# A hybrid decoder step: token tiles that overlap by 15 in the pooling mixer, compact 32x32 inverses, and an uneven final block

## The chip, the core and the metric

One core of a Trainium2 chip runs the kernel. The core has a matrix engine (TensorE, in the profile PE, with its weight loads as PEld), a vector engine (VectorE, DVE), a scalar engine (ScalarE, ACT), GpSimd (POOL), and SyncE (SP), whose queue issues the DMA transfers here. PE multiplies a stationary operand of up to 128 by 128 (the weights, loaded ahead of each product) with a moving operand and writes to PSUM, which has eight banks here. The metric is the time of one execution in microseconds of device time.

## What is computed

The reference is one step of a two-layer decoder, D = 1024, for 512 prompt tokens and 8 x 8 sample tokens (64), so T = 576 columns. All of it is float32. Cut to what matters:

```python
def pool_mixer(h, buf, w_grp, scale, n_past):
    # group g: trailing mean over POOL_WINDOWS[g] = 2, 4, 8, 16 positions minus the token,
    # then a linear map of the group's 256 channels, and a scale per channel
    ...
    diffs.append(total / count - cur[..., c0:c1])
    y = einsum('blgc,gce->blge', d, w_grp).reshape(B, L, D_MODEL)
def swiglu(h, w_in, w_out):
    gu = h @ w_in
    return (silu(gu[..., :D_FF]) * gu[..., D_FF:]) @ w_out      # D_FF = 2816
# layer 0: x += norm(pool_mixer(norm(x)));       x += norm(swiglu(norm(x)))
# layer 1: x += norm(gated_delta_net(norm(x)));  x += norm(swiglu(norm(x)))
```

A token's pooled mean needs at most the 15 tokens before it. In the gated delta net (16 value heads, chunks of 64 tokens) each chunk needs the inverse of a triangular matrix, which is built from 32x32 blocks. Besides the outputs for prompt and sample tokens, the last 15 mixer inputs, the last convolution inputs and the delta-rule states are returned.

## The kernel before, in words

The residual x is kept transposed, channels on partitions and tokens in columns, as eight tiles of 128 x 576. Weights and activations are split into a high and a low part (wh, wl; hH, hL; aH, aL; dH, dL in the mixer), both of a reduced float32 type, and each product is three: wh by the high part, wh by the low part, wl by the high part (mm3, line 979). ACT makes the high part of a weight, DVE or POOL the low one (line 971 and after; wraw is the loaded tile). Products of plain F32 operands show as two records each.

The work runs in this order.

- Mixer (from line 1227). Five token tiles are loaded (xt; four of 128 prompt tokens and one of 64 sample tokens), normed (xn), and transposed into x (residual, line 1303). The difference of mean and token is a product of xn with a band matrix: bm for a token tile, bf for the first one, bh (15 columns wide) for the tokens of the tile before that reach into this one, bs for the sample tokens and bt for their saved state rows (stp). Two halves of columns, 256 and 320 (HALVES), one in PSUM banks A and one in B; for each the four window groups one after the other (loop from line 1320).
- FFN of layer 0 (ffn, from line 1148). The gate and up products of six blocks of 128 features run for the halves 256 and 320 (gate_up), so that the second half's norm can follow; the other blocks use a Strassen scheme on halves of 288 and 288 (EVEN; its operands are ta, tb, s1h, dh and so on). The output products (out, line 1173) run after each of four blocks of features; the last block goes half by half, since the norm of a half needs all its outputs.
- Gated delta net: four groups of four heads; each is projected (ps_m), convolved, and goes through a scan with the inverses (inv32, line 1407), while the projections of the next group run. Uw holds the triangular matrices, ia and ii are the working tiles of the inverse; vt is read back from DRAM (z_d).
- FFN of layer 1, whose last block ends the kernel: the outputs yo are squared and summed (nsq, nacc), scaled with a gain (nh), turned back to token rows by PE transposes (turn_y, line 2165; yT), and added to the turned residual x (xa, xb) by a scaling on DVE with the norm's factor nrc (finish1, line 2182). PIECES says which token rows are turned together, up to 128.

The order of the instructions on all engines comes from a planner (class Plan). It records every operation with a cost from a formula, schedules the list forward and backward, and then shakes the ranks window by window with the seeds in the table CHOSEN. So any change in the operations needs a new table, and gives a new order everywhere. The planner also places filler products (ps_w, ones by ones, line 527) where it foresees that PE waits. EITHER (line 827) leaves it to the planner whether DVE or POOL does an operation. The banks of PSUM are handed out by tag in rings (RING): "A" is banks 0, 1, 2 and "B" is 3, 4, 5.

All instructions that the planner emits have one line in the profile (531, in the changed kernel 526), so the tiles' names tell them apart.

## Time and profile before

| what | us |
|---|---|
| median of 3 runs | 1526.5 (1526.38 to 1527.4) |
| profiled execution | 1525.06 |
| its span, first to last instruction | 1523.3 |
| PE busy in the span | 1501.0 |
| DVE busy | 1155.7 |
| ACT busy | 840.6 |
| POOL busy | 129.4 |

In a row of a timeline stand start, duration, engine, line, operation, out<-in with the sizes (partitions x elements), and in brackets an idle time ahead of it with what ended it. The duration of a product holds its latency; how fast products follow each other is read from their starts. In a row of a group stand the sum and the mean in ns. "x2" counts instructions that were put into one row, and the weight loads of PE have rows of their own.

### The profile page before, as it was taken

To read this page: it belongs to the slowest core of one execution; us is meant where nothing else is said; L and a number is where in the kernel's file an instruction comes from. 1 tells how busy PE (TensorE), PEld (TensorE's weight loads), DVE (VectorE), ACT (ScalarE), POOL (GpSimd) and SP (SyncE) were. 2 spreads that over 40 slices of the span, in tenths; PEclk is the share of its full clock that TensorE was granted. 3 is DMA by queue.
4 is the path that set the end of the run, shared out by engine and by line. 5 is a ranking of instruction groups with operands and counts; after the bars stand their busy time and mean duration, and the time that the engine had idled before them with its cause. 6 is when DMAs were issued, how large, how long until landed. Compare 5 with 4: busy or idle time off the path is not lost.

```text
span 1523.3 us, 30379 instructions
## 1 busy us (share of the span) xinstructions
PE 1501.0 (99%) x11850; PEld 1452.8 (95%) x11850; DVE 1155.7 (76%) x2284; ACT 840.6 (55%) x1815; POOL 129.4 (8%) x269
## 2 busy tenths in 40 slices
PE   8999999999999999999999999999999999999997
PEld 7999999999999899899899899999999999999997
DVE  6993566678688698997899799667896476766865
ACT  7753543435466975764763764545565453534553
POOL 4210000000011010121120120100110000000000
PEclk9999999999999999999999999999999999999999
DMA  6563323233457433335433544657765333233263
GB/s 190 156 188 110 98 74 111 67 99 104 148 170 204 114 88 111 102 103 147 111 112 93 147 127 128 202 158 220 240 184 155 109 87 96 83 89 110 66 196 99
DMA packets 344902, 197.86 MB, mean 130 GB/s; under 512 B 13547, under 2 KB 337740, under 8 KB 344751
## 3 DMA queue, kind: packets, MB, share of 16 engines
q1 hardware_dynamic: 344759, 195.92, 44.6%
q8 instruction: 93, 1.52, 0.4%
q14 instruction: 50, 0.41, 0.1%
HBM read 165.60 MB, written 30.52 MB: 129 GB/s over the span
## 4 chain that ended last, share of the span: by engine, by line
PE 88%; DVE 6%; ACT 3%; DMA 2%; issue 1%; POOL 0%; SPq 0%; DVEq 0%; ACTq 0%; POOLq 0%
PE ps_B L531 29%; PE ps_A L531 26%; PE ps_m L531 19%; PE ps_s L531 5%; PE ps_k L531 5%; PE ps_x L531 2%; PE ps_e L531 1%; DVE wl L531 1%; PE ps_n L531 1%; DVE Uw L531 1%; DMA vt<-z_d 1%; DVE ac L531 1%; ACT wh L531 1%; DMA wraw<-in_gdn_w_in_dram 0%; DMA yo<-y_d 0%
## 5 line engine op out<-in xcount | busy, mean ns | idle before, releaser
L531 ACT ACTIVATE wh<-wraw 128x1024 fp32r<-128x1024 f32 (+4 forms) x239 | 232.5, 978 | 201.5 <-PE ps_B L531 79.6
L531 DVE TENSOR_TENSOR wl<-wraw,wh 128x1024 fp32r<-128x1024 f32 (+4 forms) x231 | 258.3, 1122 | 76.0 <-ACT wh L531 40.3
L531 PE MATMUL ps_m<-hH,wh 128*128 128x320 f32 (+1 forms) x832 | 251.5, 313 | 0.0
L531 PE MATMUL ps_m<-hL,wh 128*128 128x320 f32 (+1 forms) x832 | 247.5, 306 | 0.1
L531 PE MATMUL ps_m<-hH,wl 128*128 128x256 f32 (+1 forms) x832 | 245.8, 308 | 0.1
L531 PEld LDWEIGHTS ps_m<-hH,wh 128*128 128x128 f32 x832 | 155.1, 190 | 4.0 <-issue 1.0
L531 PEld LDWEIGHTS ps_m<-hL,wh 128*128 128x128 f32 x832 | 156.0, 190 | 2.0 <-issue 0.8
L531 PEld LDWEIGHTS ps_m<-hH,wl 128*128 128x128 f32 x832 | 154.7, 190 | 1.7 <-issue 0.4
L531 PE MATMUL ps_B<-hH,wh 128*128 128x320 f32 (+1 forms) x444 | 127.8, 304 | 0.2
L531 PE MATMUL ps_B<-hL,wh 128*128 128x320 f32 (+1 forms) x444 | 127.1, 304 | 0.0
L531 PE MATMUL ps_B<-hH,wl 128*128 128x320 f32 (+1 forms) x444 | 127.1, 304 | 0.0
L531 PE MATMUL ps_A<-hH,wh 128*128 128x256 f32 (+1 forms) x432 | 119.4, 292 | 0.0
L531 PE MATMUL ps_A<-hL,wh 128*128 128x256 f32 (+1 forms) x432 | 117.7, 290 | 0.0
L531 PE MATMUL ps_A<-hH,wl 128*128 128x256 f32 (+1 forms) x432 | 117.5, 291 | 0.1
L531 PE MATMUL ps_B<-aL,wh 128*128 128x288 f32 x352 | 100.0, 296 | 0.0
L531 PE MATMUL ps_B<-aH,wl 128*128 128x288 f32 x352 | 99.2, 297 | 0.7 <-DVE wl L531 0.7
L531 PE MATMUL ps_B<-aH,wh 128*128 128x288 f32 x352 | 99.1, 298 | 0.5 <-DVE xa L531 0.5
L531 PE MATMUL ps_A<-aL,wh 128*128 128x288 f32 x352 | 98.3, 296 | 0.0
L531 PE MATMUL ps_A<-aH,wl 128*128 128x288 f32 x352 | 97.7, 297 | 0.0
L531 PE MATMUL ps_A<-aH,wh 128*128 128x288 f32 x352 | 97.1, 297 | 0.0
L531 PEld LDWEIGHTS ps_B<-hH,wh 128*128 128x128 f32 x444 | 81.7, 188 | 0.7 <-ACT wh L531 0.6
L531 DVE SCALAR_TENSOR_TENSOR ac<-u,cwt,ac 128x600 f32<-128x600 f32 x96 | 79.5, 837 | 3.3 <-ACT ac L531 3.1
(463 smaller groups left out, 4040.8 us busy)
## 6 DMA issues: line engine op xcount, KB each, us to landing
wraw<-in_ffn_w_in_dram SPq DMA_DIRECT2D x77, 512.0 KB
wraw<-in_gdn_w_in_dram SPq DMA_DIRECT2D x56, 512.0 KB
graw<-in_ffn_w_in_dram SPq DMA_DIRECT2D x33, 512.0 KB
wraw<-in_ffn_w_out_dram SPq DMA_DIRECT2D x32, 448.0 KB
wraw<-in_gdn_w_out_dram SPq DMA_DIRECT2D x24, 512.0 KB
wraw<-in_ffn_w_out_dram SPq DMA_DIRECT2D x32, 320.0 KB
St<-in_state_gdn_rec_dram SPq DMA_DIRECT2D x32, 256.0 KB
out_dram<-St SPq DMA_DIRECT2D x32, 256.0 KB
```

Of the source, the lines that this page charges most:

```text
L531: calls[e](*a, **k)
```

## The change

Three parts, and a new table CHOSEN with them.

1. The mixer's token tiles overlap. Tile i starts at prompt token 0, 113, 225, 338 or 448 (TILES: start, rows that only serve as history, new tokens); the last holds 64 prompt rows and the 64 sample rows. Every new token has its 15 predecessors in its own tile, so bh goes, and bs now makes the columns of the last tile, 49 prompt and 64 sample tokens. The halves of the mixer, and of the first FFN's gate and up products, become 240 and 336 (MIX). Per channel tile there are six band products instead of nine.
2. In inv32, the four transposes of 32 partitions on DVE at each end become four copies on ACT and one DVE transpose over 128 partitions, in two different orders of the two steps.
3. In the last block of the second FFN the halves are 320 and 256 (LAST), in five pieces of rows instead of six. All its output products use the banks A, and all turned y the banks B; before, the first half had outputs in A and turned y in B, and the second the other way round.

```diff
@@ -28,10 +28,13 @@
 T = SEQ + SMP
 Half = collections.namedtuple("Half", "i o n")
 HALVES = (Half(0, 0, 256), Half(1, 256, 320))
+MIX = (Half(0, 0, 240), Half(1, 240, 336))
+TILES = ((0, 0, 128), (113, 15, 112), (225, 15, 113), (338, 15, 110), (448, 15, 113))
 EVEN = (Half(0, 0, 288), Half(1, 288, 288))
 EV = 288
 KQ = NC // 2
-PIECES = (((0, 128), (128, 128), (256, 32)), ((288, 128), (416, 96), (512, 64)))
+LAST = (Half(0, 0, 320), Half(1, 320, 256))
+PIECES = (((0, 128), (128, 128), (256, 64)), ((320, 128), (448, 128)))
 DFF = 2816
 FBLOCKS = ((6, 5, 4, 7), (5, 5, 5, 7))
 AB = 7
@@ -77,207 +80,199 @@
     CHOSEN = (
-        "0: 51633 4180 93590 78750 34477 23530 63076 77272 88530 16072 91213 50029 90818 92607 6488 48788 652 "
...
+        "0: 21739 22500 52758 86855 86637 95893 57905 59345 46358; 1: 98229 52998 77840 70450 66207 3734 98530 "
...
@@ -1173,7 +1168,8 @@
         def out(bi, f0, m, hf, w):
             s = state[hf.i]
             at = slice(hf.o, hf.o + hf.n)
-            ps = bank("AB"[hf.i])[:, :hf.n]
+            ends = turn is not None and bi == len(blocks) - 1
+            ps = bank("A" if ends else "AB"[hf.i])[:, :hf.n]
             mm3(ps, w, lambda k: tuple(v[:, at] for v in acts[f0 + k]), blocks[bi])
@@ -1216,7 +1212,7 @@
                         out(bi, f0, m, hf, w)
-                for hf in EVEN:
+                for hf in EVEN if turn is None else LAST:
                     for m in range(NC):
                         out(bi, f0, m, hf, wts.load(wout, f0 * P, m * P, nb))
                     finish(hf, state[hf.i]["acc"])
@@ -1234,10 +1230,12 @@
             def load_x(tt):
-                n = P if tt < SPANS else SMP
-                xts[tt] = ip.tile([P, D], F32, name="xt", tag="xt", bufs=3)[:n]
-                SP.dma_start(xts[tt], x_prompt[0, tt * P:(tt + 1) * P] if tt < SPANS
-                                  else x_sample.rearrange("b t d -> (b t) d"))
+                t0 = TILES[tt][0]
+                n = min(P, SEQ - t0)
+                xts[tt] = ip.tile([P, D], F32, name="xt", tag="xt", bufs=3)
+                SP.dma_start(xts[tt][:n], x_prompt[0, t0:t0 + n])
+                if n < P:
+                    SP.dma_start(xts[tt][n:], x_sample.rearrange("b t d -> (b t) d"))
@@ -1262,18 +1260,16 @@
-                h_ = ip.tile([P, POOL_BUF], F32, name="bh%d" % g)
-                POOL.memset(h_, 1.0 / win)
-                POOL.affine_select(h_, h_, [[-1, POOL_BUF]], ALU.is_ge, 0.0, base=win - 1 - P, channel_multiplier=1)
-                bh.insert(0, h_)
             for g in (3, 2, 1, 0):
                 win = 2 << g
-                s_ = ip.tile([SMP, SMP], F32, name="bs%d" % g)
-                DVE.tensor_tensor(s_.rearrange("p (b t) -> p b t", b=NB),
-                                  bm[g][:SMP, :SMP].rearrange("p (b t) -> p b t", b=NB),
-                                  seqm.unsqueeze(2).to_broadcast([SMP, NB, NT]), op=mult)
+                s_ = ip.tile([P, P - POOL_BUF], F32, name="bs%d" % g)
+                EITHER.tensor_copy(s_[:, :SMP - POOL_BUF], bm[g][:, POOL_BUF:SMP])
+                POOL.memset(s_[:SMP, SMP - POOL_BUF:], 0.0)
+                DVE.tensor_tensor(s_[SMP:, SMP - POOL_BUF:].rearrange("p (b t) -> p b t", b=NB),
+                                  bm[g][SMP:, SMP:].rearrange("p (b t) -> p b t", b=NB),
+                                  seqm2[SMP:].unsqueeze(2).to_broadcast([SMP, NB, NT]), op=mult)
@@ -1286,27 +1282,26 @@
...
+                n = min(P, SEQ - TILES[tt][0])
+                DVE.tensor_scalar(xn[:n], xt[:n], st_[:n], None, op0=mult)
+                if n < P:
+                    DVE.scalar_tensor_tensor(out=xn[n:], in0=xt[n:], scalar=st_[n:], in1=grow[n:], op0=mult, op1=mult)
+                    SP.dma_start(np_sample[0, :, POOL_BUF - NT:POOL_BUF], xn[n:])
             def residual(tt, hi):
-                n = P if tt < SPANS else SMP
+                t0, r, n = TILES[tt]
                 for c4 in range(0, NC, 4):
                     px = bank("AB"[hi], (P, 4, P))
                     for c in range(4):
-                        PE.transpose(px[:, c, :n], xts[tt][:, (c4 + c) * P:(c4 + c + 1) * P], ident[:n, :n])
-                    ACT.activation(x[:, c4:c4 + 4, tt * P:tt * P + n], px[:, :, :n], AF.Copy)
+                        PE.transpose(px[:, c], xts[tt][:, (c4 + c) * P:(c4 + c + 1) * P], ident)
+                    ACT.activation(x[:, c4:c4 + 4, t0 + r:t0 + r + n], px[:, :, r:r + n], AF.Copy)
@@ -1352,20 +1348,20 @@
                         ps = bank(tag)
-                        for tt in mine[:2]:
-                            o = tt * P - o0
-                            PE.matmul(ps[:, o:o + P], xns[tt][:, cs], bm[g] if tt else bf[g], start=True, stop=tt == 0)
-                            if tt:
-                                PE.matmul(ps[:, o:o + POOL_BUF], xns[tt - 1][:, cs], bh[g], start=False, stop=True)
+                        for tt in mine:
+                            t0, r, k = TILES[tt]
+                            o = t0 + r - o0
+                            band = bf[g] if tt == 0 else bs[g] if tt == SPANS else bm[g][:, r:r + k]
+                            PE.matmul(ps[:, o:o + k], xns[tt][:, cs], band, start=True, stop=tt < SPANS)
+                        if hi == 1:
+                            PE.matmul(ps[:, np_:n], stp[:, cs], bt[g], start=False, stop=True)
                         gn = prm[:, G_MPRE + c:G_MPRE + c + 1]
-                        ACT.activation(dH[:, j, :256], ps[:, :256], AF.Copy, scale=gn)
-                        DVE.scalar_tensor_tensor(out=dL[:, j, :256], in0=ps[:, :256], scalar=gn,
-                                                 in1=dH[:, j, :256].bitcast(F32), op0=mult, op1=sub)
+                        ACT.activation(dH[:, j, :np_], ps[:, :np_], AF.Copy, scale=gn)
+                        DVE.scalar_tensor_tensor(out=dL[:, j, :np_], in0=ps[:, :np_], scalar=gn,
+                                                 in1=dH[:, j, :np_].bitcast(F32), op0=mult, op1=sub)
                         if hi == 1:
-                            PE.matmul(ps[:, 256:n], xns[SPANS][:, cs], bs[g], start=True, stop=False)
-                            PE.matmul(ps[:, 256:n], stp[:, cs], bt[g], start=False, stop=True)
-                            ACT.activation(dH[:, j, 256:], ps[:, 256:n], AF.Copy)
-                            DVE.tensor_tensor(dL[:, j, 256:], ps[:, 256:n], dH[:, j, 256:].bitcast(F32), op=sub)
+                            ACT.activation(dH[:, j, np_:], ps[:, np_:n], AF.Copy)
+                            DVE.tensor_tensor(dL[:, j, np_:], ps[:, np_:n], dH[:, j, np_:].bitcast(F32), op=sub)
@@ -1410,11 +1406,12 @@
         XT = ap_.tile([P, 2, 512], F32, name="ii", tag="ii", bufs=1)
+        D32 = XT[:, 1].rearrange("p (i h) -> p i h", h=16)
         for b in range(4):
             s = slice(32 * b, 32 * b + 32)
-            DVE.transpose(A[s], W[s, :, 32 * b:32 * b + 32].rearrange("p h i -> p i h").unsqueeze(2)
-                          .to_broadcast([32, 32, 2, 16]))
-            yield 1.2
+            ACT.activation(D32[s], W[s, :, s].rearrange("p h i -> p i h"), AF.Copy)
+        DVE.transpose(A, D32.unsqueeze(2).to_broadcast([P, 32, 2, 16]))
+        yield 1.2
         EITHER.tensor_copy(X, eye2)
         for m in range(31, 0, -1):
@@ -1423,10 +1420,10 @@
             DVE.tensor_tensor(X[:, :m, lo:], X[:, :m, lo:], tv, op=sub)
             yield 2 * (m * (16 - lo) + 60) / 700
+        DVE.transpose(XT[:, 1].rearrange("p (i j) -> p i j", j=32), X.rearrange("p j i -> p i j"))
         for b in range(4):
             s = slice(32 * b, 32 * b + 32)
-            DVE.transpose(W[s, :, 32 * b:32 * b + 32].rearrange("p h (i d) -> p i d h", d=2),
-                          X[s].rearrange("p j i -> p i j"))
+            ACT.activation(W[s, :, s].rearrange("p h i -> p i h"), D32[s], AF.Copy)
             yield 0.6
@@ -2168,10 +2165,10 @@
...
             for i, (o, n) in enumerate(PIECES[hf.i]):
                 if c % 4 == 0:
-                    yT[o, c // 4] = bank("BA"[hf.i], (P, 4, P))[:n].rearrange("p c f -> p (c f)")
+                    yT[o, c // 4] = bank("B", (P, 4, P))[:n].rearrange("p c f -> p (c f)")
                 ps = yT[o, c // 4]
@@ -2184,22 +2181,23 @@
...
-            last = PIECES[hf.i][2][1]
+            whole = hf.n // P
-                n = n if i == 2 else P
-                a = acc[0]
-                PE.matmul(ps[:n, i:i + 1], a[:, i * P:i * P + n] if i < 2 else a[:, EV - n:], ones[:, 0:1],
-                          start=True, stop=True)
-            for r, q in ((slice(0, P), slice(0, 2)), (slice(0, last), slice(2, 3))):
-                ACT.activation(rc[r, q], ps[r, q], AF.Sqrt, bias=eps_c[r], scale=1.0 / D)
-                DVE.reciprocal(rc[r, q], rc[r, q])
+                PE.matmul(ps[:n, i:i + 1], acc[0][:, o - hf.o:o - hf.o + n], ones[:, 0:1], start=True, stop=True)
+            for r, q in ((slice(0, P), slice(0, whole)), (slice(0, hf.n % P), slice(whole, whole + 1))):
+                if r.stop:
+                    ACT.activation(rc[r, q], ps[r, q], AF.Sqrt, bias=eps_c[r], scale=1.0 / D)
+                    DVE.reciprocal(rc[r, q], rc[r, q])
...
```

The rest is of the same kind: ffn takes its halves as an argument (the second one keeps 256 and 320), and the last 15 prompt rows come from the last tile.

The order of instructions moves with it. First PE in the middle of the last block, where the first half of the outputs ends and the second starts. Before:

```order
L531 MATMUL ps_n_3745<-ones,nacc 128x1 x2
L531 MATMUL ps_B<-ident,nh 128x128
L531 MATMUL ps_n_3745<-ones,nacc 32x1
L531 MATMUL ps_B<-ident,nh 128x128
L531 MATMUL ps_B<-ident,nh 32x128
L527 MATMUL ps_w<-ones 128x128 x5
L531 MATMUL ps_B<-ident,nh 128x128 x2
L531 MATMUL ps_B<-ident,nh 32x128
L531 MATMUL ps_B<-ident,nh 128x128 x2
L531 MATMUL ps_B<-ident,nh 32x128
L527 MATMUL ps_w<-ones 128x128 x2
L531 MATMUL ps_B<-aH,wh 128x288
```

After, from the last products of the first half (320 columns) on; before these rows 256-wide products stand mixed with 320-wide ones from 25 rows earlier on:

```order
L526 MATMUL ps_A<-aH,wl 128x320
L526 MATMUL ps_A<-aH,wl 128x256 x2
L526 MATMUL ps_A<-aH,wh 128x256 x2
L526 MATMUL ps_A<-aL,wh 128x256 x2
L526 MATMUL ps_B<-ident,nh 128x128
L526 MATMUL ps_A<-aH,wl 128x256 x2
L526 MATMUL ps_A<-aH,wh 128x256
L526 MATMUL ps_B<-ident,nh 128x128
L526 MATMUL ps_A<-aH,wh 128x256
L526 MATMUL ps_B<-ident,nh 64x128
```

The filler products (ps_w) are gone here, and the transposes of nh stand between products of the second half; the norm products (ps_n<-ones,nacc) of the first half come some 60 rows later.

Then DVE at the first of the four inverses. Before, and after:

```order
L531 STREAM_TRANSPOSE ia<-Uw 32x1024
L531 TENSOR_TENSOR QD<-ps_k,QD 128x2x128
L531 STREAM_TRANSPOSE ia<-Uw 32x1024 x3
L531 TENSOR_TENSOR ks<-ps_k,ks 64x128
L531 TENSOR_TENSOR ii<-ia,ii 128x31
L531 TENSOR_TENSOR ks<-ps_k,ks 64x128
L531 TENSOR_TENSOR ii<-ii 128x31
```

```order
L526 TENSOR_TENSOR vt<-ps_x,nk 128x4x128
L526 STREAM_TRANSPOSE ia<-ii 128x1024
L526 TENSOR_TENSOR ks<-ps_k,ks 64x128
L526 TENSOR_TENSOR ii<-ia,ii 128x31
L526 COPY nct<-u 128x24
L526 TENSOR_TENSOR ii<-ii 128x31
```

Four transposes into ia are one, and its source is now ii, which ACT has filled with four copies of 32x512 from Uw.

Last PE where the mixer turns from the first half of the columns (banks A) to the second (banks B). Before:

```order
L531 MATMUL ps_A<-dL,wh 128x256
L531 MATMUL ps_A<-dH,wl 128x256
L531 MATMUL ps_A<-dL,wh 128x256
L531 MATMUL ps_A<-dH,wl 128x256
L531 MATMUL ps_B<-bm_142,xn 128x128
L531 MATMUL ps_B<-bh_144,xn 128x15
L531 MATMUL ps_B<-bm_142,xn 128x128
L531 MATMUL ps_B<-bh_144,xn 128x15
L527 MATMUL ps_w<-ones 128x128 x2
L531 MATMUL ps_B<-bs_154,xn 128x64
L531 MATMUL ps_B<-bt_155,stp 128x64
L531 MATMUL ps_B<-bs_154,xn 128x64
```

After:

```order
L526 MATMUL ps_B<-bm_142,xn 128x113
L526 MATMUL ps_B<-bm_142,xn 128x110
L522 MATMUL ps_w<-ones 128x128 x4
L526 MATMUL ps_n_235<-ones,nacc 128x1 x2
L526 MATMUL ps_B<-ident,xt 128x128 x8
L522 MATMUL ps_w<-ones 128x128 x2
L526 MATMUL ps_n_238<-ident,nrc 128x128
L526 MATMUL ps_n_238<-ident,nrc 128x112
L526 MATMUL ps_B<-bm_142,xn 128x113
L526 MATMUL ps_B<-bm_142,xn 128x110
L522 MATMUL ps_w<-ones 128x128 x5
L526 MATMUL ps_B<-bs_150,xn 128x113 x2
```

Before, the band products of the second half stood among products of the first, with two fillers ahead of the sample products; now none of them stands there, and 11 of 14 new fillers stand in these rows, three more just behind them.

## The prediction

> **What bounds the kernel now.** I read the page first (busy shares, then the chain that ended last), then the busy time by 40 us windows, then the filler products by stage, and last the rows of the places that the change touches.

> ```profile
> PE 1501.0 (99%) x11850; PEld 1452.8 (95%) x11850; DVE 1155.7 (76%) x2284; ACT 840.6 (55%) x1815; POOL 129.4 (8%) x269
> PE 88%; DVE 6%; ACT 3%; DMA 2%; issue 1%; POOL 0%; SPq 0%; DVEq 0%; ACTq 0%; POOLq 0%
> ```

> TensorE (PE) is busy nearly all the time, and 88% of the chain is its own work. So time can come from two places only: fewer or cheaper products, and the stretches where PE has nothing to do. The windows show where those stretches are (columns: length, then PE busy, weight loads, DVE, ACT, POOL, then the granted clock; the 520 us row is the delta net as a whole).

> ```profile
> 0.00:40.00 40.00, 34.34 (x233) 31.71 (x234) 27.02 (x78) 30.08 (x74) 18.82 (x78) 0.91 0.65 181
> 40.00:80.00 40.00, 39.94 (x322) 39.05 (x321) 38.28 (x89) 28.92 (x61) 8.39 (x9) 1.00 0.61 182
> 440.00:960.00 520.00, 513.34 (x4344) 479.87 (x4342) 458.66 (x1086) 334.36 (x913) 83.24 (x161) 1.00 0.44 125
> 760.00:800.00 40.00, 39.63 (x283) 37.87 (x283) 38.23 (x96) 27.14 (x73) 9.71 (x16) 1.00 0.37 107
> 1240.00:1280.00 40.00, 40.00 (x304) 39.99 (x303) 24.39 (x42) 14.45 (x22) 0.00 (x0) 1.00 0.31 90
> 1480.00:1520.00 40.00, 33.69 (x250) 31.16 (x248) 23.93 (x42) 19.91 (x39) 0.00 (x0) 1.00 0.34 106
> ```

> The FFN windows such as 1240 to 1280 are full: only the product count and width matter there. The start loses 5.7 us, the end 6.3 us (and the tail after it), and the delta net 6.7 of 520, some tenths in each window, with DVE at 38 of 40 in the fuller ones. Busy time also hides waiting, because the plan puts filler products (ps_w) where it expects PE to wait. By stage:

> ```profile
> 0.00:80.00 80.00, 3.62 (x16) 3.16 (x16) 0.96 0.63 181
> 440.00:960.00 520.00, 7.72 (x48) 6.72 (x48) 1.00 0.44 125
> 1480.00:1523.30 43.30, 3.06 (x20) 2.68 (x20) 0.96 0.35 109
> ```

> An F32 product is two records, so these are 8, 24 and 10 fillers, which are waits that do no work.

> **The change, part by part.** The sum is made against the profiled execution (1525.06 us, span 1523.3), which is 1.4 us below the median of the three runs, 1526.5; I add the sum to the median.

> *Mixer.* The 24 products over a second tile (bh) go, and the eight sample products (bs), 64 rows deep before, become 128 deep and 113 wide. Rows (start, duration):

> ```profile
> 31.58 0.43 PE L531 MATMUL ps_B<-bs,xn 64*128 64x64 f32 x2
> 31.94 0.44 PE L531 MATMUL ps_B<-bt,stp 120*128 120x64 f32 x2
> 32.19 0.39 PE L531 MATMUL ps_B<-dH,wh 128*128 128x320 f32 x1
> 33.96 0.29 PE L531 MATMUL ps_B<-bh,xn 128*128 128x15 f32 x2
> 34.09 0.47 PE L531 MATMUL ps_B<-bm,xn 128*128 128x128 f32 x2
> 34.32 0.39 PE L531 MATMUL ps_B<-dL,wh 128*128 128x320 f32 x1
> ```

> From start to start a bh takes 0.13 us, a bm 0.23, a bs 0.36. So 24 x 0.13 = 3.1 us go with the bh, and 8 x (0.36 - 0.23) = 1.0 with the bs, if it now costs what a bm does. The narrower bm I leave at their price. Wider transposes of the last tile give back about 0.3 (eight of 128 by 128, 0.11 each, for eight of 64). So 3.8 us of PE work go. But the order now plans 25 fillers up to the second half of the first FFN against 8: 14 of them stand where the first half of the mixer has ended and the second waits for its band matrices and its last token tile, 4 where the FFN turns to its second half. At the price of a filler, 0.22 us (two records; their spacing is shown below), the 17 more are 3.7 us. The shorter work is planned to end up as waiting, since norms, copies and splits on ACT (30.08 of 40 us) and DVE (38.28) set when operands are ready; ten small instructions more (bs copies, memsets, the last tile's norm) go to DVE and POOL ahead of it. Net -0.1; bounds: -3.8 if the waits turn out empty, +4 if each lasts twice its fillers and the work saved is no help.

> *Halves 240 and 336 instead of 256 and 320*, in 48 mixer and 288 FFN pairs. No product of this 3-term kind narrower than 256 columns is in the trace. Its neighbours:

> ```profile
> 65.09 0.28 PE L531 MATMUL ps_A<-hH,wh 128*128 128x256 f32 x1
> 65.81 0.28 PE L531 MATMUL ps_A<-hH,wh 128*128 128x256 f32 x1
> 44.15 0.31 PE L531 MATMUL ps_B<-dH,wl 128*128 128x320 f32 x1
> 45.03 0.34 PE L531 MATMUL ps_B<-dL,wh 128*128 128x320 f32 x1
> 1513.72 0.73 PEld L531 LDWEIGHTS ps_n<-ones,nacc 128*128 128x128 f32 x6
> ```

> Six steps each: 0.72 us for 256 columns (120 ns), 0.88 for 320 (147 ns); at 288 the window 1240 to 1280 has 304 in 40 us (132 ns). That is a line of 0.42 ns a column, so 336 takes 153.7 and 240 takes 113.3 ns, together the same 267 as before. The other bound is that 120 is a floor: +6.7 ns x 336 = +2.3 us. The last row shows weight loads (0.19 each) about 108 ns apart, (0.73 - 0.19) / 5, which is under 113, so I lean to the line: +0.5, range 0 to +2.3.

> [...]

> *Compact inverses*, four times (one for each head group):

> ```profile
> L531 DVE STREAM_TRANSPOSE ia<-Uw 32x1024 f32<-32x1024 f32 x16 | 32.6, 2034 | 0.2
> L531 DVE STREAM_TRANSPOSE Uw<-ii 32x512 f32<-32x512 f32 x16 | 18.2, 1138 | 0.4
> L531 ACT ACTIVATE Rs<-ps_k 32x512 f32<-32x512 f32 x8 | 4.7, 589 | 8.3 <-PE ps_k L531 8.1
> L531 DVE TENSOR_TENSOR wl<-wraw,wh 128x1024 fp32r<-128x1024 f32 x151 | 184.4, 1225 | 39.4 <-ACT wh L531 22.9 <-PE ps_B L531 7.8 <-PE ps_A L531 7.2
> L531 POOL TENSOR_TENSOR wl<-wraw,wh 128x1024 fp32r<-128x1024 f32 x8 | 19.3, 2414 | 18.5 <-ACT wh L531 18.5
> DVE vt L531 <- DMA vt<-z_d: 12.4, 4, 5.2
> ```

> DVE loses 50.8 us and gets 4 x (2.03 + 1.14) = 12.7 back if a transpose over 128 partitions costs what one over 32 does (four times as much at the other end, then it wins nothing: the columns decide in the rows, 1024 against 512, so I take the first). It also takes the eight weight splits from POOL, 8 x 1.23 = 9.8. Net -28 us on DVE. ACT gets 32 copies of 32x512, 32 x 0.59 = 19 us. The chain of one inverse gets 4 x 2.03 + 4 x 1.14 = 12.7 before to 3.2 + 8 x 0.59 = 7.9, nearly 5 us shorter. PE is hidden behind none of this directly: it works on projections meanwhile. What it can win is its waits from 440 to 960. The new order plans 12 fillers there instead of 24, 12 x 0.22 = -2.7 us, and I take that. Bounds: +4 (a new order meets its waits elsewhere, ACT's copies delay a weight's high part, wh, for which DVE's wl and then PE wait), and -8 (fillers and half the open waits go). Not all can go: vt waits for a DMA, as the last row shows.

> *Uneven final block.* Turning x and y takes 40 transposes each instead of 48: 16 x 0.11 = -1.7. Its 168 product pairs, 132 + 132 before, are now 147 + 120: +0.5. The middle of the block:

> ```profile
> 1481.95 0.76 PE L531 MATMUL ps_B<-ident,nh 128*128 128x128 f32 x2 [0.20 <-ACT yT L531]
> 1482.54 0.39 PE L527 MATMUL ps_w<-ones 128*128 128x128 f32 x2
> 1484.46 1.28 PE L527 MATMUL ps_w<-ones 128*128 128x128 f32 x10
> 1486.51 0.97 PE L531 MATMUL ps_B<-ident,nh 128*128 128x128 f32 x6 [0.77 <-ACT nh L531]
> 1487.32 0.61 PE L527 MATMUL ps_w<-ones 128*128 128x128 f32 x4
> 1488.40 0.40 PE L531 MATMUL ps_B<-aH,wh 128*128 128x288 f32 x1 [0.47 <-DVE xa L531]
> 1484.48 1.28 ACT L531 ACT_TABLE_LOAD   x1
> ```

> (Ten filler records take 1.28 us, one 0.28: 0.11 apart, 0.22 for two.) The second half's products go to bank B, which the turned y of the first half holds until DVE has scaled it, behind a table load on ACT. From about 1481.4, the last first-half product, to 1488.40 PE does some 15 transposes and 3 short products, 2.1 us, in 7.0 us. Now all products go to bank A and all turned y to B, and the order has the 256-wide products mixed with the last 320-wide ones, with the transposes and norm products of the first half among them: -4.9. What hides the norm and its scaling is now the second half, 168 x 0.12 = 20.2 us of PE, over which DVE has six weight splits (about 1.0 each), eight adds and seven squares (0.4) and six scalings (0.7), some 16 us. It fits, but not by much; where it does not, bank A comes late and -3 is left. Range -3 to -6.

> *Tail.*

> ```profile
> 1512.12 0.46 DVE L531 TENSOR_TENSOR yo<-yo,ps_B 128x288 f32<-128x288 f32 x1 [1.63 <-PE ps_B L531]
> 1514.87 0.30 DVE L531 RECIPROCAL nrc<-nrc 128x2 f32<-128x2 f32 x2 [1.26 <-ACT nrc L531]
> 1518.38 0.73 DVE L531 SCALAR_TENSOR_TENSOR xb<-ps_A,nrc,xb 64x512 f32<-64x512 f32 x1
> ```

> Four scalings of about 0.66 us instead of six after the reciprocal: -1.3. Against it, two scalings of the first half, three nh and one yT now stand ahead of the last norm, +0.7, and the last piece leaves by two DMAs: -0.3, range -1 to +1.

> Sum: -0.1 + 0.5 - 2.7 - 1.7 + 0.5 - 4.9 - 0.3 = -8.7. So 1516.4 from the profiled run, 1517.8 from the median.

> **The rivals.** *Slower by the narrow products.* If a 3-term product under 256 columns runs like an F32 pass, the change loses. Their speeds:

> ```profile
> 613.02 0.59 PE L531 MATMUL ps_k<-S,qk 128*128 128x256 f32 x2
> 613.45 0.61 PE L531 MATMUL ps_s<-rs,Uw 128*128 128x128 f32 x4
> ```

> An F32 product of 256 columns takes 0.43 us in its two passes, 3.6 times the 120 ns. At that rate 240 columns take 0.40 us, +0.29 x 336 = +96 us: about 1614. At one pass it is 0.20, +29 us: about 1547. It decides from 113 + 8.7 / 336, that is from 139 ns on. For it: nothing under 256 is in the trace. Against it: 256, 288 and 320 lie on one line that shows no limit close by. Chance 0.08.

> *Slower by the new order of the delta net.* Every window from 440 to 960 is ordered anew, with DVE at 38 of 40 us before, 19 us more on ACT and 10 us of splits from POOL. If PE there waits 0.7 us more in each of 13 windows (+9, about the 6.7 us of open waits there again), the sum is 2.7 + 9 = 12 higher: about 1529.5 and more, 1531 typically. Against it: fewer fillers are planned there, and DVE has 28 us less. Chance 0.12.

> *No change: the gain is given back.* The start takes +4 and the delta net 0, and the middle gives 3: -8.7 + 4.1 + 2.7 + 1.9 = 0. For it: the band work saved is planned as waiting already, and a wait by plan was longer in the trace at the start (5.7 us open beside the fillers). That gives 1526.5. Chance 0.14.

> *More than forecast.* Empty waits at the start (-3.7 more) and -8 in the delta net: about 1509. Chance 0.04.

> **How the numbers follow.** The forecast, with 0.62, is 1517.8, with 1510 to 1523 as its own range. 3 us, 0.2%, is about what a measurement of this kernel can tell from no change. Faster: 0.62 + 0.04 = 0.66. Within: 0.14. Slower: 0.08 + 0.12 = 0.20. The range from 1510 to 1531 leaves out the narrow-product case, half of the re-ordered one and most of the fourth, and holds about 0.82.

> **What would show it.** The spacing of the 240-column products: 113 to 120 ns. The transpose ia over 128 partitions: near 2.0 us, and DVE's sum lower by about 28 us. In the middle of the last block no gap over 1 us on PE, and the last window's PE near 39 of 40 up to the last product. From 440 to 960 open waits and fillers together down from 12 us (6.7 open, 24 x 0.22) to about 9. Before the second half of the mixer a wait of 3 to 4 us with fillers in it. I am wrong if the narrow products take over 139 ns, if bank A makes PE wait in the last block, or if the delta net's windows lose more than before.

## The result: no change, and the profile after

| | runs | median, us | range, us |
|---|---|---|---|
| before | 12 | 1526.81 | 1525.01 to 1529.23 |
| changed | 12 | 1527.98 | 1524.97 to 1531.29 |

The ratio is 1.0008, 95% interval 1.0001 to 1.0016. That is within 0.2%, where 1517.8 (0.6% less) was forecast. The profiled execution of the changed kernel took 1530.85 us (span 1529.1), at the upper end of its runs, so a second trace of it is used beside it (below; span 1524.9, time 1526.59).

Page of the changed kernel, busy shares and the chain of waits:

```profile
PE 1497.1 (98%) x11778; PEld 1451.5 (95%) x11778; DVE 1131.1 (74%) x2278; ACT 865.4 (57%) x1839; POOL 104.2 (7%) x249
PE 82%; DVE 8%; ACT 5%; issue 3%; DMA 2%; POOL 0%; SPq 0%; DVEq 0%; ACTq 0%; POOLq 0%
```

PE is busy for 3.9 us less, but in a span that is 5.8 us longer. ACT has grown by 24.8 us where I gave it 19: its 32 new copies take 35.7 (below), and other rows fell, table loads by 5.1 (26 instead of 30). Its share of the chain has grown by 2 points. Busy time by windows (length, then PE, weight loads, DVE, ACT, POOL, clock, DMA):

```profile
0.00:40.00 40.00, 33.76 (x228) 30.51 (x229) 30.38 (x91) 30.70 (x79) 17.55 (x73) 0.96 0.70 187
240.00:280.00 40.00, 38.13 (x277) 37.94 (x276) 24.12 (x37) 13.51 (x20) 0.00 (x0) 0.96 0.32 93
440.00:960.00 520.00, 504.99 (x4213) 474.97 (x4212) 430.50 (x1070) 354.17 (x925) 59.87 (x149) 0.99 0.43 121
640.00:680.00 40.00, 37.03 (x254) 35.58 (x254) 36.39 (x106) 28.61 (x74) 4.22 (x9) 0.96 0.37 107
1480.00:1520.00 40.00, 39.44 (x307) 38.62 (x306) 26.22 (x46) 23.03 (x43) 0.00 (x0) 1.00 0.47 142
```

The delta net row (440 to 960) now leaves 15.0 us open, 6.7 before, and there are windows with a clock under 1.00 that had 1.00 before. The last row and its row of before (33.69 of 40) hold different lengths of the tail, so the last block is better compared up to its last output product, the changed kernel first:

```profile
1480.00:1516.45 36.45, 36.45 (x286) 36.25 (x285) 23.54 (x41) 21.07 (x38) 0.00 (x0) 1.00 0.48 141
1480.00:1511.79 31.79, 29.88 (x224) 28.41 (x223) 18.77 (x32) 15.94 (x30) 0.00 (x0) 1.00 0.36 111
```

It is filled: nothing is open there, where 1.9 us were, beside 16 filler records that are gone. The fillers by stage moved as planned, 42 records (before 16) at the start, 24 (48) in the delta net, 4 (20) at the end:

```profile
0.00:80.00 80.00, 7.35 (x42) 6.50 (x42) 0.98 0.69 196
440.00:960.00 520.00, 3.74 (x24) 3.21 (x24) 0.99 0.43 121
1480.00:1529.10 49.10, 0.77 (x4) 0.60 (x4) 0.92 0.47 142
```

To place the difference I read three starts from each trace: the first and the last projection product of the delta net (ps_m<-hH,wh), and the last output product of the second FFN. The table gives each stage's length less that of before, in us; the last three columns are kernels of the next section. The medians are compared with runs of before from the same set: 1526.81 here, and 1526.31, 1526.17 and 1525.95 in the three sets of experiments.

| stage | predicted | changed | changed, second trace | contiguous copies | old inverses | final block alone, second |
|---|---|---|---|---|---|---|
| up to the delta net's first product | +0.4 | +3.1 | +1.5 | -0.3 | +4.2 | -0.5 |
| delta net | -2.7 | +9.3 | +6.8 | -4.5 | +0.5 | +0.5 |
| second FFN, to its last product | -6.1 | -7.7 | -7.7 | -7.3 | -6.2 | -5.3 |
| after it | -0.3 | +1.2 | +1.1 | +0.9 | +1.0 | +1.2 |
| span | -8.7 | +5.8 | +1.6 | -11.1 | -0.5 | -4.2 |
| medians of the runs | | +1.2 | +0.6 | -9.0 | -5.4 | -5.1 |

So the gain of the last block came, and the delta net took it back. What stands at a wait there, first PE, then ACT, then DVE, in the first trace of the changed kernel:

```profile
667.37 0.60 PE L522 MATMUL ps_w<-ones 128*128 128x128 f32 x4
669.93 0.66 PE L526 MATMUL ps_x<-ident,ac 128*128 128x128 f32 x4 [1.96 <-ACT ac L526]
663.42 4.52 ACT L526 ACTIVATE ii<-Uw 32x512 f32<-32x512 f32 x4 [0.24 <-DVE Uw L526]
667.96 1.28 ACT L526 ACT_TABLE_LOAD   x1
669.25 0.63 ACT L526 ACTIVATE ac<-ac 128x512 f32<-128x512 f32 x1
667.97 1.25 DVE L526 STREAM_TRANSPOSE ia<-ii 128x1024 f32<-128x1024 f32 x1 [1.55 <-ACT ii L526]
```

Four copies of an inverse hold ACT for 4.52 us in one piece. Behind them in ACT's queue stand a table load and the activation ac, for which PE waits 1.96 us after two fillers. In the delta net as a whole PE now waits for ACT's u, ac and Uw, 8.1 us together; before, its only wait for ACT there was the last row (total, times, longest, in us):

```profile
PE ps_m L526 <- ACT u L526: 3.3, 4, 1.8
PE ps_x L526 <- ACT ac L526: 2.6, 2, 2.0
PE ps_k L526 <- ACT Uw L526: 2.2, 4, 0.8
PE ps_x L531 <- ACT nco L531: 0.2, 1, 0.2
```

The groups show why (mean in ns):

```profile
L526 DVE STREAM_TRANSPOSE ia<-ii 128x1024 f32<-128x1024 f32 x4 | 5.0, 1246 | 5.0 <-ACT ii L526 5.0
L526 DVE STREAM_TRANSPOSE ii<-ii 128x512 f32<-128x512 f32 x4 | 4.3, 1077 | 0.1
L526 ACT ACTIVATE ii<-Uw 32x512 f32<-32x512 f32 x16 | 17.9, 1117 | 0.4 <-DVE Uw L526 0.2
L526 ACT ACTIVATE Uw<-ii 32x512 f32<-32x512 f32 x16 | 17.8, 1110 | 6.8 <-DVE ii L526 6.5
```

A copy takes 1.11 us. I had taken 0.59, and the order is planned for copies of 0.63, the planner's price (contiguous ones took 0.627, below): each run of four is some 1.9 us later than planned, which is the length of the wait. These copies read or write one float every 512 bytes ("p h i -> p i h").

### The profile page after: what moved, and what is told of

Its sections match the earlier page's. It is cut to its first block, busy times and chain, and to the rows that moved or that the text cites. A ratio compares the mean times of both kernels' runs of the same rounds, so it can differ in the third digit from the quotient of the medians.

```text
span 1529.1 us, 30269 instructions
## 1 busy us (share of the span) xinstructions
PE 1497.1 (98%) x11778; PEld 1451.5 (95%) x11778; DVE 1131.1 (74%) x2278; ACT 865.4 (57%) x1839; POOL 104.2 (7%) x249
## 4 chain that ended last, share of the span: by engine, by line
PE 82%; DVE 8%; ACT 5%; issue 3%; DMA 2%; POOL 0%; SPq 0%; DVEq 0%; ACTq 0%; POOLq 0%
PE ps_B L526 27%; PE ps_A L526 25%; PE ps_m L526 16%; PE ps_s L526 4%; PE ps_k L526 4%; PE ps_x L526 2%; PE ps_e L526 2%; DVE wl L526 1%; ACT ii L526 1%; DMA wraw<-in_ffn_w_in_dram 1%; PE ps_n L526 1%; DVE y L526 1%; ACT Uw L526 1%; DVE ii L526 1%; DMA vt<-z_d 1%
## 5 line engine op out<-in xcount | busy, mean ns | idle before, releaser
L526 PE MATMUL ps_m<-hH,wl 128*128 128x320 f32 (+1 forms) x832 | 244.1, 309 | 0.0
L526 PE MATMUL ps_B<-hH,wh 128*128 128x288 f32 (+2 forms) x444 | 127.0, 306 | 0.2 <-ACT wh L526 0.2
L526 PE MATMUL ps_B<-hL,wh 128*128 128x288 f32 (+2 forms) x444 | 127.1, 305 | 0.0
L526 PE MATMUL ps_B<-hH,wl 128*128 128x288 f32 (+2 forms) x444 | 126.6, 305 | 0.3 <-DVE wl L526 0.3
L526 PE MATMUL ps_A<-hH,wh 128*128 128x288 f32 (+2 forms) x432 | 120.0, 289 | 0.4 <-ACT wh L526 0.3
L526 PE MATMUL ps_A<-hH,wl 128*128 128x288 f32 (+2 forms) x432 | 119.4, 288 | 0.0
L526 PE MATMUL ps_A<-hL,wh 128*128 128x288 f32 (+2 forms) x432 | 119.1, 288 | 0.0
L526 PE MATMUL ps_A<-aH,wh 128*128 128x288 f32 (+2 forms) x408 | 113.6, 298 | 1.9 <-DVE y L526 1.9
L526 PE MATMUL ps_A<-aH,wl 128*128 128x288 f32 (+2 forms) x408 | 113.4, 299 | 0.0
L526 PE MATMUL ps_A<-aL,wh 128*128 128x288 f32 (+2 forms) x408 | 113.1, 297 | 0.0
```

What stands on the lines that cost most here:

```text
L526: calls[e](*a, **k)
```

## The experiments

Theory 1: the strided copies hold ACT, and through it PE, and the clock. Theory 2: the new order of the delta net loses as such, whatever the copies take. In all experiments but the first the planner is left out, and the order is written down as a list: that of the changed kernel as it is, or the orders of both kernels joined stage by stage by their planned starts.

```diff
-    CHOSEN = (
+    ORDER = (
...
+        for w in self.ORDER.split():
+            if w[0] == "f":
+                b, k = w[1:].split(".")
+                best[1].append(((int(b), int(k)), None))
+            else:
+                best[1].append((int(w[1:]), {"p": "PE", "a": "ACT", "d": "DVE", "o": "POOL", "s": "SP"}[w[0]]))
```

**The changed kernel once more.**

> The changed kernel once more, for a second trace. If its loss is in its order and in the four copies on ACT at each inverse, the waits stand at the same places as in the first trace (PE idle about 1.9 us near 558 and 670 us, behind four copies of 1.1 us in a row), and the granted clock is down after them; the time is 1525 to 1531. If the waits of the first trace were an accident of that run, other places show them, and the time is at the lower end, 1525.

Median 1526.89 us, ratio 1.0004 (0.9992 to 1.0017). The second trace has the same waits, 1.84 us at 555 and 1.96 us at 666 us, so they are the kernel's. What differs is how often the clock fell behind them. Stretches of 5 us, the first trace, then the second:

```profile
250.00:255.00 5.00, 4.73 (x24) 4.76 (x25) 2.74 (x6) 1.06 (x1) 0.00 (x0) 0.66 0.72 206
670.00:675.00 5.00, 5.00 (x27) 4.96 (x28) 4.70 (x14) 2.65 (x8) 0.33 (x2) 0.66 0.15 30
```

```profile
250.00:255.00 5.00, 5.00 (x39) 5.00 (x38) 3.82 (x7) 1.06 (x1) 0.00 (x0) 1.00 0.69 205
665.00:670.00 5.00, 4.07 (x31) 4.07 (x32) 4.59 (x15) 3.63 (x10) 0.33 (x2) 1.00 0.05 13
```

Behind the wait of 1.96 us the granted clock had a mean of 0.66 over 5 us in the one execution and stayed at 1.00 in the other. By an estimate, a slice at 0.66 costs 5 x 0.34 = 1.7 us. From 80 us to the last output product the first trace has four such slices (at 251, 538, 558 and 671 us), the second one (at 555 us), before and the contiguous copies below none; the mean clock over the span is 0.992, 0.995, 0.997 and 0.997 in the four traces. Three slices, 5.1 us, are enough for the 4.3 us between the two traces, and such slices are likely behind much of the changed kernel's spread. The waits cost time without them too: with one slice in it, the second trace's delta net is still 6.8 us longer than before.

The wait near 250 us lies in the first FFN, and it is another one. DVE stands 6.5 us before a weight load, with a weight split and y behind it (the DVE row, then the PE row, first trace). The load is hardly later than before, where the same DVE instruction starts at 245.87 us; but the first FFN has begun 4.3 us earlier (46.42 us against 50.74), and here a part of that lead is lost:

```profile
246.28 0.69 DVE L526 TENSOR_TENSOR s1raw<-wraw 128x512 f32<-128x512 f32 x1 [6.50 <-DMA wraw<-in_ffn_w_in_dram]
250.27 0.37 PE L526 MATMUL ps_A<-aH,wh 128*128 128x288 f32 x1 [1.86 <-DVE y L526]
```

**The copies contiguous, every instruction in its place.**

```diff
-        D32 = XT[:, 1].rearrange("p (i h) -> p i h", h=16)
+        D32 = XT[:, 1].rearrange("p (h i) -> p h i", h=16)
-            ACT.activation(D32[s], W[s, :, s].rearrange("p h i -> p i h"), AF.Copy)
-        DVE.transpose(A, D32.unsqueeze(2).to_broadcast([P, 32, 2, 16]))
+            ACT.activation(D32[s], W[s, :, s], AF.Copy)
+        DVE.transpose(A, D32.rearrange("p h i -> p i h").unsqueeze(2).to_broadcast([P, 32, 2, 16]))
...
-        DVE.transpose(XT[:, 1].rearrange("p (i j) -> p i j", j=32), X.rearrange("p j i -> p i j"))
+        DVE.transpose(D32.rearrange("p h (i d) -> p i d h", d=2), X.rearrange("p j i -> p i j"))
-            ACT.activation(W[s, :, s].rearrange("p h i -> p i h"), D32[s], AF.Copy)
+            ACT.activation(W[s, :, s], D32[s], AF.Copy)
```

> The changed kernel with every instruction in the same place on every engine; only the layout in which the 32 copies on ACT put their data is another (rows of 32 stay contiguous on both sides), and the DVE transposes read and write that layout. Theory 1, the strided copies (1.11 us measured, 0.63 in the plan's price) hold ACT and so PE: a copy takes about 0.6 us, the waits near 558 and 670 us shrink from 1.9 to under 0.5 us, the clock stays at 1.00, and the time falls by 5 to 9 us, to 1519 to 1523. Theory 2, the new order of the delta net as such loses: no more than 2 us are gained, 1526 to 1528.

Median 1517.29 us (1511.75 to 1519.89), ratio 0.9933 (0.9914 to 0.9952). Groups, and the delta net's window:

```profile
L961 ACT ACTIVATE Uw<-ii 32x512 f32<-32x512 f32 x16 | 10.0, 627 | 6.9 <-DVE ii L961 6.6
L961 ACT ACTIVATE ii<-Uw 32x512 f32<-32x512 f32 x16 | 10.0, 627 | 0.4 <-DVE Uw L961 0.2
L961 DVE STREAM_TRANSPOSE ia<-ii 128x1024 f32<-128x1024 f32 x4 | 8.2, 2043 | 0.1
```

```profile
440.00:960.00 520.00, 512.61 (x4426) 481.65 (x4425) 437.83 (x1077) 349.56 (x950) 60.21 (x148) 1.00 0.45 128
```

The same order with copies of 0.63 us is 9.6 us faster than the second set of the changed kernel's runs (1526.89). Open time in the delta net falls from 15.0 to 7.4 us, and the clock is 1.00. The DVE transpose pays for it, since it now does the strided reading (2.04 us instead of 1.25), but once for 128 partitions, where before four of 32 partitions took 2.03 each. Theory 2 falls: this order is good when the copies take what it was planned for. This kernel is faster than both. A caution on the size: its trace reaches the delta net 1.7 to 3.3 us earlier than the changed kernel's two, where no instruction differs yet; near 250 us PE waits 0.23 us in it, and 1.86 and 1.25 in the two. The delta net alone is 11.3 to 13.8 us shorter.

**The first four copies of each inverse contiguous, the last four strided.**

```diff
+        C32 = XT[:, 1].rearrange("p (h i) -> p h i", h=16)
-            ACT.activation(D32[s], W[s, :, s].rearrange("p h i -> p i h"), AF.Copy)
-        DVE.transpose(A, D32.unsqueeze(2).to_broadcast([P, 32, 2, 16]))
+            ACT.activation(C32[s], W[s, :, s], AF.Copy)
+        DVE.transpose(A, C32.rearrange("p h i -> p i h").unsqueeze(2).to_broadcast([P, 32, 2, 16]))
```

> The changed kernel, every instruction in its place, with only the first four copies of each inverse (16 of 32, from Uw into ii) in contiguous rows; the last four (from ii back to Uw) stay strided. The waits of 1.8 to 2.0 us near 555 and 666 us stand behind the first four, those of 0.8 us near 593 and 710 us (products of T and Uw) behind the last. If each copy costs PE what it delays, the first four bring the larger part of the 9 us that all 32 brought: 1519 to 1521. If only the sum of ACT's time counts, half: 1522.

Median 1522.42 us, ratio 0.9974 (0.9965 to 0.9983): 4.5 of the 9.6 us, half. The runs of four on ACT at the second inverse:

```profile
661.04 2.56 ACT L961 ACTIVATE ii<-Uw 32x512 f32<-32x512 f32 x4 [0.24 <-DVE Uw L961]
705.65 4.49 ACT L961 ACTIVATE Uw<-ii 32x512 f32<-32x512 f32 x4
```

The waits at 555 and 666 us are gone. I had expected more from the first four, by the size of the waits that show on PE. The last four cost as much. Directly PE waits only 2.2 us for them in the changed kernel (the rows of ps_k<-T,Uw, ACT Uw above). In this trace, which was the slowest of its runs, the clock also had a lower mean in the delta net, 0.99, than with all copies contiguous (1.00); where the rest of their cost lies is not shown.

**The changed kernel with the old inverses.** inv32 as before, the delta net in the order of before, all else in the order of the changed kernel.

> The changed kernel with the old inverses (16 + 16 transposes on DVE, no copies on ACT), the delta net in the order of the kernel before, the mixer, both FFNs and the end in the order of the changed one. If the delta net's loss comes from the copies alone, the rest of the change keeps its gain of about 7 us in the second FFN and the end, less 1 for the end of the first FFN and up to 3 for the seams where the two orders meet: 1519 to 1523. If the compact inverses are needed for the gain, 1525 or more.

Median 1520.82 us, ratio 0.996 (0.9947 to 0.9973): 6 us faster than with the strided copies, and 3.5 us slower than with the contiguous ones. So the compact inverses with the order that was planned for them are a gain of about 3.5 us with contiguous copies, and a loss of about 6 with strided ones. The gain is the less certain of the two: the intervals of the two ratios overlap a little (up to 0.9952, from 0.9947), and with the old inverses there are joins between the two orders, with 2.2 us of waits at the first (before 0.8 there). How much is due to the inverses themselves and how much to the order isn't separated.

**The uneven final block alone, twice.** The kernel before with LAST, PIECES and the bank tags of the diff. In the first run the 40 transposes of x stood where the changed kernel's plan has them; in the second where the first 40 corresponding ones of before stood.

> The kernel before with the uneven final block alone; up to that block all instructions stand as before. Read off the two traces, the stretch from the first Strassen product of the second FFN to the last output product became 9.3 us shorter, and what follows 1.2 us longer: 1518 to 1520. The prediction's terms for this part (-4.9 - 1.7 + 0.5 - 0.3) make 6.4, so 1520.4. If the gain belongs to the re-planned FFN rather than to the block, 1523 or more.

Median 1525.16 us, ratio 0.999 (0.9981 to 0.9999). PE waited about 2.5 us among the transposes of x, and the Strassen part ended 4.9 us late. That was how the two orders had been joined.

> The kernel before with the uneven final block alone, as in the first such run, but the 40 transposes of x now stand where the first 40 of the 48 corresponding ones stood; in the first such run they were packed into a shorter stretch, PE waited about 2.5 us among them, and the Strassen part ended 5 us late. If that was what hid the gain, 1519 to 1522 (the prediction's terms for this part make -6.4). If the block itself gains no more than it did there, 1525.

Median 1521.06 us, ratio 0.9963 (0.9951 to 0.9975). With the transposes where they belong the block gives 5.1 us alone, near the 6.4 of the prediction's terms.

**The overlapping tiles alone, twice.** The kernel before with the first part of the diff; the mixer and the first FFN in the changed kernel's order.

> The kernel before with the overlapping token tiles and the halves 240 and 336 alone, these and the first FFN in the order of the changed kernel, all from the delta net on in the order of before. If the early end of the mixer (the first FFN product 4.3 us earlier in the changed kernel) counts, 1522 to 1524. If the first FFN gives it back, as the first trace has it (2.97 us late at the end of the first FFN, with a wait of 1.86 us at 250 us and a slower clock after it), 1526 to 1530; without that one wait about 1525.

Median 1548.17 us, ratio 1.0138 (1.012 to 1.0156). This is the join again: from 500 to 524 us PE alternated between small gate products (ps_g) and projections, and the first mark after it, the products of gts, came 15.1 us late (at 542.6 us). Nothing is said by it about the tiles.

> The kernel before with the overlapping tiles and the halves 240 and 336 alone, the mixer and the first FFN in the order of the changed kernel, the rest in that of before; the seam now lies behind the last output product of the first FFN (in the first such run it lay behind products of the delta net, which left the small gate products, ps_g, mixed with projections, and cost some 15 us there). The prediction's terms for this part make +0.4. By the stage marks of the other runs the first FFN ends between 0.4 us earlier and 3.2 us later than before, and the seam may cost up to 3: 1526 to 1531. Below 1523 this part would be a gain that the other runs hide.

Median 1529.16 us, ratio 1.0022 (1.0013 to 1.0031). The first FFN ends 1.7 us late, with the wait at 250 us (1.09 us there), and PE waits 2.1 us at the new join (before 0.8). So this part brings no gain here; how much of the 3.2 us is its own, and how much the join's, stays open. The kernel with the old inverses holds this part and the uneven block, with the same kind of join, and gained 5.4 us, where the block alone gained 5.1. By that the tiles cost nothing; by this run up to 3.2 us.

## Why the prediction was wrong

- **The delta net is the term that failed.** Predicted -2.7, bounds -8 and +4; measured +9.3 and +6.8 in the two traces. The step is "32 copies of 32x512, 32 x 0.59 = 19 us", priced by the row Rs<-ps_k. That row writes runs of 32 floats, the copies of the diff step by 512 bytes at each element. They take 32 x 1.11 = 35.7 us. With that one price put right by the contiguous copies (0.63 us), the delta net came to -4.5, and the kernel to 1517.29 us, where 1517.8 was forecast; that the two agree so closely is partly luck, since the start, the last block and the tail each missed by about 1 us, in both directions. I wrote that ACT's copies could delay the high part of a weight, and put +4 on it; the place was ACT, but what PE waited for was ac, u and Uw, behind runs of four copies that I had counted one by one. One of the prediction's own signs of being wrong came true: open time and fillers from 440 to 960 us are 15.0 + 2.6 = 17.6 us, where 9 was expected, and 12 were there before. (The term itself, 12 x 0.22, is 2.6 and not 2.7, which changes nothing.) The plan's own price had the same error, so fewer fillers were no evidence that fewer waits would come.
- The transposes were misjudged the other way: 1.25 us for the first, where I had taken 2.03, since its source is now contiguous. The stride had moved from DVE, which paid for it in before's 2.03, to ACT. DVE fell by 24.6 us (predicted 28) although its transposes came out cheaper, since some 8 us of other small work came to it beside the weight splits. What the stride costs can be read from the two layouts: (2043 - 1246) / 1024 = 0.78 ns more per element for DVE's transpose, and (1117 - 627) / 512 = 0.96 ns more for ACT's copy.
- **The mechanism of the last block was right.** Predicted -6.1 for the second FFN; measured -7.7, -7.3 with contiguous copies, -6.2 with the old inverses, -5.3 alone. Where PE stood idle there is now a mix of halves without a gap (PE's timeline of the changed kernel, first trace, as in the next two fences):

```profile
1497.21 0.27 PE L526 MATMUL ps_B<-ident,nh 128*64 128x128 f32 x1
1497.23 0.37 PE L526 MATMUL ps_A<-aL,wh 128*128 128x256 f32 x1
1497.44 0.27 PE L526 MATMUL ps_B<-ident,nh 128*128 128x128 f32 x1
1497.46 0.63 PE L526 MATMUL ps_A<-aH,wl 128*128 128x320 f32 x3
```

- **The narrow products were right.** The row below and one four products later: 0.44 us for four, 0.11 each (predicted 0.113), so the rival of +29 to +96 us falls. The pair costs no more than before: 240 columns follow at 112 ns and 336 at 154 in the median, 266 together, where 256 and 320 made 267.

```profile
60.06 0.27 PE L526 MATMUL ps_A<-hH,wh 128*128 128x240 f32 x1
60.50 0.27 PE L526 MATMUL ps_A<-hL,wh 128*128 128x240 f32 x1
```

- **The start came out worse than predicted,** though within its wide bounds: +0.4 predicted, +1.5 to +4.2 in the traces, but for the -0.3 with contiguous copies. The work saved did come back as planned waits, 42 filler records instead of 16. The wait for a weight load in the first FFN I hadn't looked for.
- **The tail went the other way.** Predicted -0.3, measured +0.9 to +1.2. The last product starts at 1516.45, and the end is 12.7 us behind it, 11.5 before. DVE's reciprocal comes 4.1 us after that product (before 3.1, from 1511.79 to 1514.87), with two scalings of the first half and the nh and yT ahead of it, and the four scalings after it wait for yT and transposes instead of following each other, so they save 0.5 us and not 1.3. From the end of the last scaling to the end of the kernel it is 4.9 us, before 4.2; the last piece has 128 rows in two DMAs now, 64 in one before. The three are +1.0 - 0.5 + 0.7 = +1.2:

```profile
1516.45 0.28 PE L526 MATMUL ps_A<-aH,wl 128*128 128x256 f32 x1
1520.55 0.17 DVE L526 RECIPROCAL nrc<-nrc 128x2 f32<-128x2 f32 x1 [1.38 <-ACT nrc L526]
1520.75 0.75 DVE L526 SCALAR_TENSOR_TENSOR xa<-yT,nrc,xa 128x512 f32<-128x512 f32 x1
1521.83 0.75 DVE L526 SCALAR_TENSOR_TENSOR xb<-yT,nrc,xb 128x512 f32<-128x512 f32 x1 [0.33 <-ACT yT L526]
1522.82 0.75 DVE L526 SCALAR_TENSOR_TENSOR xa<-ps_B,nrc,xa 128x512 f32<-128x512 f32 x1 [0.24 <-PE ps_B L526]
1523.48 0.74 DVE L526 SCALAR_TENSOR_TENSOR xb<-ps_B,nrc,xb 128x512 f32<-128x512 f32 x1
```

- Of the rivals, "the gain is given back" had the right time (1526.5) for the wrong places: it put the loss at the start and in the last block. The one on the delta net had the right place, and a price (+12 against the sum) near what came, for a general reason instead of the copies.

## What to carry to other kernels

A row prices an instruction only if its access pattern is the same: here the copy of 32x512 took 1.11 us with a step of 512 bytes and 0.63 in runs of 32, the transpose to 128x1024 took 2.04 with a step on its source and 1.25 without. So before taking a duration for a copy that rearranges, look at which side steps and how far, and ask which engine paid for the stride before. When an order was planned by a price, an instruction that takes longer than its price also delays what stands behind it in its queue, and several of them in a row add up, even on an engine with time to spare: here 32 x 0.48 = 15 us more on ACT, which is busy for 57% of the span, cost the kernel 9.6 us. Where one change has several parts, a run that keeps every instruction in its place and changes only the duration in doubt tells the price from the order.

## What the runs showed of the hardware

```profile
667.67:671.08 3.41, 1.45 (x12) 1.26 (x11) 2.78 (x9) 3.38 (x8) 0.33 (x2) 1.00 0.44 126
671.08:674.49 3.41, 3.41 (x16) 3.37 (x15) 3.31 (x8) 1.57 (x4) 0.00 (x0) 0.50 0.09 19
```

```profile
664.34:667.75 3.41, 1.82 (x14) 1.82 (x15) 3.01 (x11) 3.40 (x8) 0.33 (x2) 1.00 0.25 76
667.75:671.16 3.41, 3.41 (x27) 3.40 (x26) 3.38 (x8) 0.89 (x3) 0.00 (x0) 1.00 0.25 61
```

In the first trace the whole wait lies in one step, PE was busy for 1.45 of its 3.41 us, and the next step is slow. In the second, 0.37 us of the wait lie in the step before, PE was busy for 1.82 us, and no step is slow. From 20 to 1505 us of the first trace, PE was busy for less than half of a step at full clock three times, for 1.55, 1.57 and 1.45 us from 247.83, 555.03 and 667.67 us, and a slow step followed each; the fourth slow step followed one with 2.44 us, from 534.55. Behind steps with 2.43 us (from 712.04) and 1.95 (from 848.58) none was slow, nor behind one with 2.17 us in the trace of before (from 1485.62). This was read off afterwards and no run was made to test it; the steps with 2.44 and 2.43 us show that PE's busy share alone doesn't settle it.

Chance shows in the clock at the start too. Clock and PE from 12 to 16 us with contiguous copies, then with the old inverses, where this stage has the same order:

```profile
12.00:16.00 4.00, 4.00 (x27) 3.96 (x26) 2.97 (x9) 3.06 (x8) 1.81 (x8) 0.70 0.99 303
```

```profile
12.00:16.00 4.00, 3.71 (x15) 3.35 (x16) 2.96 (x6) 2.36 (x7) 1.83 (x7) 0.50 0.91 337
16.00:20.00 4.00, 4.00 (x28) 4.00 (x27) 2.33 (x11) 3.25 (x9) 0.00 (x0) 0.71 1.18 264
```

In the second the clock rose some 4 us later, and the first dH product of the second half started at 35.0 us instead of 32.8. Single traces of these kernels can so differ by 2 to 4 us that no edit made (2.2 here, 4.3 between the two of the changed kernel), which is why the medians stand beside the stage table.
